# Threshold attention on one core: the spare products that keep the array's clock become single steps of a searched order, the start's warming products become smaller, and the order is searched on

## The chip, the cores and the metric

The kernel runs on 1 core of one Trainium2 chip. The metric is the device time of one execution in microseconds. The engines are PE (TensorE, the matrix products, with PEld for its weight loads), ACT (ScalarE), DVE (VectorE), POOL (GpSimd) and SP (SyncE, which here only issues DMAs). Each engine works through its own instructions in the order of the program; they wait for each other by semaphores.

## The reference

Q, K and V are float32 of 8 batches x 12 heads x 512 rows x 64. The weights of a row that are over a threshold of 0.1 are kept and divided by their sum, the others are zero:

```python
scores = np.einsum('bhqd,bhkd->bhqk', Q, K) * scale
weights = np.exp(scores - np.max(scores, axis=-1, keepdims=True))
weights = weights / (np.sum(weights, axis=-1, keepdims=True) + 1e-10)
weights = np.where(weights > threshold, weights, 0)
weights = weights / (np.sum(weights, axis=-1, keepdims=True) + 1e-10)
return np.einsum('bhqk,bhkd->bhqd', weights, V).astype(np.float32)
```

With 512 keys and a softmax over random scores, few rows have any weight over 0.1, and such a row mostly has one. The kernel is built on that.

## The kernel before

The 96 heads are taken as 48 pairs (`hp`), 24 groups of four heads (`hq`) and 12 groups of eight (`j`). The work has two parts.

The **body** looks in low precision for rows that might have a weight over the threshold. In the names that the planner and this text use:

- `k(hp)` and `q(hq)` load K (two DMAs from SP, L194) and Q (one DMA from POOL's queue, L209, which casts to f16). `z(hq)` clears four heads of the output in HBM with one DMA from SP (L324); every output row that is not written later stays zero.
- `ktr`, `kev`, `kf` transpose K on PE (L334), copy it from PSUM (L317 on ACT, L319 on DVE) and cast it to f16 (on POOL, L321). `qmix`, `qtr`, `qev` reorder Q (POOL L321 or DVE L319), transpose it (L367) and copy it back.
- `qk(hp, c)` (L377) makes a quarter of the scores of a pair, `exp(hp, c)` their exponentials, on ACT (L383) or by an integer trick on DVE (L385).
- `d(hp, jj)` (L389) and `dred` (L399, DVE) test whether a row has an exponential that is large against the row's sum.
- `ksq`, `qsq`, `size` (L357, L412) bound the rows' norms.

The **exact rows** are done once for each group of eight heads: `flags`, `rank`, `key`, `oh`, `idx`, `half`, `idxev` number the flagged rows, up to 32 in each pair of heads; `gather` fetches their Q rows from HBM by an indirect DMA of POOL (all indirect DMAs are at L190); `split` (L463), `xtr` (L469), `xev`, `xqk` (L481, exact scores in f32), `xexp` (L489), `tv`, `found` (L500) and `vidx` (L507) find the key; `vzero` (L514), `fetch` and `scatter` bring its V row and write it to the output. For the last group all this stands behind the last exp, as a chain. After the last group `check0` and `check1` (L535 to L541) decide whether a slow, complete path is needed; it is not for these inputs.

The **order** of all this is a table. Each step is added to a `Schedule` with the engines that may do it, an occupation and a latency for each, what it depends on, and which buffers it takes and gives. `ORDER` holds two strings: the first names the steps by pairs of digits in the order in which they are emitted, the second says which engine does a step that has a choice. An order search outside of the kernel wrote them. Each engine gets its steps in the order of the table, and nothing else orders the engines: on the chip a step starts when the engine reaches it and its semaphores allow it. The planner's dependencies that stand for no data (a `k` load behind `exp(hp - 6, 0)`, a clear behind a certain exp) are not waits on the chip.

Two things of the planner matter below. PSUM and the larger SBUF tiles are held buffers (`BUFS`: 3 of `sc`, 2 of `sm`, 7 of `kt`, 3 of `kf` and so on); the small tiles of the exact rows come from rotating pools (`small` with 6, `work` with 2), which the planner did not know of.

`spare(n)` emits n products of a zero tile with itself, 128x128 by 128x512, into the first `sc` buffer, that nothing reads. There are `WARM = 7` at the start, while the first loads are under way, and `HOLD = (0, 2, 8)` more: two behind `rank` of the last group and eight behind `xqk` of the last group but one.

```python
def spare(n, buf=held["sc"][0]):
    for i in range(n):
        at = slice(i % 2 * S, (i % 2 + 1) * S)
        keep(nc.tensor.matmul(buf[:, at], lhsT=warm[:, 0:P], rhs=warm[:], start=True, stop=True))
```

In the table of before, PE's order at the end is `d(47, 7)`, four `size`, `rank(11)` with two spares, `idx(11)`, `xtr(10)`, `xtr(9)`, `xqk(10)` with eight spares, `xqk(9)`, `xtr(11)`, `xqk(11)`. POOL's is `gather(9)`, `gather(10)`, `scatter(6)`, `split(9)`, `gather(11)`, `vzero(9)`, `scatter(7)`, `vidx(10)`, `vzero(10)`, `fetch(10)`, `vzero(11)`, `scatter(8)`, `fetch(9)`, `fetch(11)`, `scatter(10)`, `scatter(9)`, `scatter(11)`.

Of the kernel before, what the change touches and what calls it, by code (L numbers as in the profile page):

```python
# [55 lines left out]
def kernel(  # L56
# [59 lines left out]
    def by_pairs(ap):  # L116
# [9 lines left out]
    WARM = 7  # L126

    HOLD = (0, 2, 8)

    ORDER = (  # L130
        "04020001060D0B050t0u08070v2021090L0J0P0C0M0K0E220G0A0Q0F030s0H0r0y0+0N0a0c0O0b0d0x0R0S0T0U0V0z0W0X0Y0e0g102n2o0Z"
        "111c0-0h0f24121K2p1526281d25160i0j190k0l272B1A171R0m0n130o0p181S0q29142A1P1L1B1Q1M2T3y2s1C1N1D1E1O1F1G1H1I2W2E1T"
        "1U1V1W1X1Y1Z2X2F1a2C2r2t2a2D2u2l2m1J1b1e2v2b2y2w2I2J2x1f1g2G2U1h2V2H1i2-1j2Y332K2L2M2N2O2P2Q2R302Z343x4h3w0I4i1k"
        "1l4j3-413E1m2z312S1n1o3X3W2c2d433+2+32443H402e2f3F35363738393A3B3C3I424f3G3D5s1p453J3L4l2g3K2h4n2i462j3M4p4m4o4N"
        "1q4s582k3N3O3P3Q4847494C4A3R3S3T4q3U4D4B4r3V4S4O4U4E4F4T4P4V4G4H4I1r1s5q6b235r0w2q6c4J4v4K1t4L5D1u5v3Y4g5x6d1v4w"
        "4M5E5u4Q5z3Z5w4t3a3b3c4R1w5R5+3d5y4u3e1x1y5-6H1z3f4W4X5B4z4Y4Z4a4b4x3g1+5C4+3h6a3i4y605F4c4d594-5051615G4e525354"
        "5566645A6765565H5I5J5K5L6f625M5N5O6h6K5Q6Z6g576i5P636k6L6j3j7m8X5S6l68696A6B6C6D6I6O6M6E6F5T7K6G6m3k725U5V5W5X3l"
        "6J6P6N6n795Y3m7k8V7l4k8W3n7A5Z7p6o3o5a6r6t6p6s6q5b5c3p6u3q7r6Q7t6R7o6S7q6T77736U7s9g5d1-7v3r7u7L786V6W6v6X756w6x"
        "6y6z6+6-707476807w7y817x8a6Y717z8c3s8B3t5e7B7C7D7E7F7G7H7+7I8e8Z8C7-8D7J8f8b8G825f83848586875g8HAP9eAQ9f3z5h8889"
        "5i8d8U8T8A9j8g5m7M9l8I8E8l7N9n7O8J8F5jAR8y9o8j7P8h8m8k5k8i5l5nBa8z7Q8K8L8M8n7R8N8O8P8Q8R8-8+3u5o7S8S7T8o909i919k"  # L140
        "8p7U8q9m8r8sAT938t8u8v92949p8wAV9u9w9F7V7WANAU9E8x9vAWAX9x95969798999A9B9C7XA59D9q9sACAY9r9tAD9GAaAsAZ9H9IA8A69J"
        "9K9L9yAA9z9+A77nBZ5t8YBYCJCKA99M7Y9-AfAx7ZA0A1A2A3ABAyAgAO7aB89NA47bAhAbAv7cAiAEAFAGAH9OAIAJAKAdAcAwAeBcAtBeCLB9"
        "Bd3v9PBf9QAuDUBhALAzAMBiDSDTBgCNCPA+9RBjB-CO7dCICRAjAkAlAmBmBkA-AnBqB0B1B2BnBrAoB3C0B4B5B67eBl7gCQEFCU7f9SCmB7Bo"
        "C2ApAqCSC1BpArC3CTC6BsBtBuBvBwBxByBz9T9UCXCV9VCY9W9hEDEECM6eC77hDXBA9aDZ9XCWB+CHCZDWCpDYBBCaCqDa9YFO5p9ZDdDv9bBC"
        "BDC4BEBFCnCbDbC5BGD2DcBH7i9cCcCoC8C9CACBCCCtCDCECdCFCGCeCfDeDgCgBICuDfBJEIBKD3EKBLDiDhDjChCiEHCrEJCjCkEMClCsELDk"
        "DwCvCwCxCyENEODlCzC+C-D0D1DxEBE0ETDmDnDoD4EgE1EUDpD5D6D7EnEREoFNFMASG7G8EjDqDrDsDtD8ESEkDuFRG9BMEPD+BND9EVBOEQDA"
        "FTDBEzBPFVDyD-EWBQDzFWFQEhEiFSFUHGHHDCEXEYEZElGBEaGDEbEcEdEeEmEyBRDDGCDEBSBU7jHI9dFXGEDFFpBTEfGFEpEqFcFYFeGGECG5"
        "GHGIBVBWFdFZFfErEsFaEtEuEvEwE2FqE3E4E5FbExGsFrE6FsFwFgE7E8E9FhFiFjFkFlFmFnHLEAE+FoI3HNGaDGFxFtFuGJFvHPE-F0F1GbGN"
        "HQGKGOHKF2DHF3HMDIGcF4GfGPFyDJFzHOGQI1JBJAI2DKF5H-GgDLG6JCHRHjI6I8F+F-GLGhG0G1G2F6HUGMGiF7F8HVGdG3G4DMGeGRGSGTGU"
        "HSGVGWHYHkGjGkGlHTGXGmGYGnGoGpGqHoHlHZHpGtGZI5IAHmI7GrF9JzDODNIBI9JFGuJHICIUFAHnGvHWGwJJGxGyGzHqIFHXHrIGJKIDG+Im"  # L150
        "I0IEHaHbHcHdHeHfHgJEFBHhIXIVJGHiIWG-FCIYJIJyJxI4DVL5BbL4FDHsFEHtIJIHIZHuHvH0HwIKFFH1InH2IIIaFIBXDPK0JLJdL6H3K2Hx"
        "HyIbJiHzILIMINIOIPIQIRISJMIcJjFGFHH+JvFJJNITJQIdIeIfJgIgIhIiIjIkJ-FKDQJRJhIlIoLtJOK1JSK4IpJPK3K5IqJeJkIrK6JTJfJl"
        "IsJUJVJWJXJYJZJaJbKOLrL7LsJ+LuFPEGGAJDHJKPKBK9KQL9H4LBKgJwJcKAItJmJnJoJpJqJrJsJtK7KCIuJuL8KVK8LAKWLDH5KDLCKELFH6"
        "LEKTKRH7KUKSH8KFKGLGLILMKXKHKYKIKJKKKZKaKLKMKbKcLHLJLNLXLwHCH9LpKhHALqKNHBLyHDLvLKLxLLL+LYLzLZL-KdLaLeLOLPKeLQLc"
        "LRHELbKfLfM0MIKiLSLTLUM7MLLVKjMaIvLWLdM8MMKkKlM1M3IwKmKnM2M4IxKoKpIyM5MPLgLhLiLjLkLlLmLnKqMNLoM6MQKrMJKsMOM9IzKt"
        "DRI+MKMAMBMCMDMEMFMGMRMbMHMSMTMUMVMWMXMYMdMZMeMfMgMcMhMiMjKuMkKvMlMmKwI-KxM+J0KyKzJ1K+MnJ6FLMoJ2MpMqK-L0L1MwHFJ3"
        "MrL2J4J5J7MsMtMuJ8MvM-MxL3MyJ9Mz",
        "0000011111100000001100001000100000011011010000100000100110000010000000100101100101000100011001000000000100011000"
        "0100001100000101000011000100000000111000110101100001000101100001000100000111010000100100000010110000111000100001"
        "1100001001010000000101100000110110011000001000000010000000001110011000000001000010000000010010000100000000100010"  # L160
        "00001010001001100011001111",
# [14 lines left out]
    sched = Schedule(BUFS)  # L176
# [86 lines left out]
    spare(WARM)  # L263

# [212 lines left out]
    def do_xqk(j, eng):  # L477
        xq = T.pop(("xq", j))
        for n in range(4):
            sl = slice(n * SLOTS, (n + 1) * SLOTS)  # L480
            keep(nc.tensor.matmul(buffer("sm", ("xs", j))[sl, :], lhsT=xq[:, sl], rhs=pair("kt", 2 * j + n // 2)[:, n % 2],  # L481
                                  start=True, stop=True, tile_position=(0, n * SLOTS)))
        if j == NO - 2:
            spare(HOLD[2])
# [80 lines left out]
    for hq in range(NQ):  # L565
# [29 lines left out]
        for n, hp in enumerate(pairs):  # L595
# [31 lines left out]
        stage("flags", {"POOL": (0.25, 0.4), "DVE": (0.12, 0.3)}, [("dred", 4 * j + n) for n in range(4)] + ["casts"], do_flags)  # L627
        for n in range(4):
# [9 lines left out]
        stage("half", {"DVE": (0.08, 0.24), "ACT": (0.2, 0.36)}, [("idx", j)], do_half)
        stage("idxev", {"DVE": (0.13, 0.30)}, [("half", j)], do_idxev, gives=[("sm", ("ix", j))])
        stage("gather", {"POOL": (1.45, 4.2 if near else 6.4, 0.1)}, [("idxev", j)], do_gather)  # L640
        stage("split", {"POOL": (0.4, 0.55), "DVE": (0.21, 0.37)}, [("gather", j), ("half", j)], do_split)
        stage("xtr", {"PE": (0.17, 0.40)}, [("split", j)], do_xtr, takes=[("sm", ("xp", j))])
        stage("xev", {"DVE": (0.2, 0.35), "ACT": (0.2, 0.36)}, [("xtr", j)], do_xev, gives=[("sm", ("xp", j))])
# [121 lines left out]
```

## Time and profile before

| | |
|---|---|
| median of 3 runs | 201.56 us (200.13 to 201.98) |
| the profiled execution | 202.59 us |
| its span in the profile | 200.9 us |
| busy: PE, DVE, ACT, POOL | 180.6, 171.3, 165.5, 120.5 us |
| mean granted TensorE clock | 0.974 |
| DMA | 32.83 MB, 163 GB/s over the span |

Times in the profile count from the start of the span. The profiled execution is one of its own beside the three runs, 1.03 us over their median. Of a line of a timeline the first number is the start, the second how long it took, then engine, line of the kernel, operation, the tiles written and read, and how many instructions are merged; brackets give the engine's idle time before it and what ended it. SPq marks the issue of a DMA, not its transfer.

### The profile page before, as it was taken

To read this page: it belongs to the slowest core of one execution; us is meant where nothing else is said; L and a number is where in the kernel's file an instruction comes from. 1 tells how busy PE (TensorE), PEld (TensorE's weight loads), DVE (VectorE), ACT (ScalarE), POOL (GpSimd) and SP (SyncE) were. 2 spreads that over 40 slices of the span, in tenths; PEclk is the share of its full clock that TensorE was granted. 3 is DMA by queue.
4 is the path that set the end of the run, shared out by engine and by line. 5 is a ranking of instruction groups with operands and counts; after the bars stand their busy time and mean duration, and the time that the engine had idled before them with its cause. 6 is when DMAs were issued, how large, how long until landed. Compare 5 with 4: busy or idle time off the path is not lost. (4 is left out here: it accounts for less than half of the span.)

```text
span 200.9 us, 7649 instructions
## 1 busy us (share of the span) xinstructions
PE 180.6 (90%) x3190; PEld 119.7 (60%) x3191; DVE 171.3 (85%) x329; ACT 165.5 (82%) x197; POOL 120.5 (60%) x191
## 2 busy tenths in 40 slices
PE   7688999999999999999999999999999897988700
PEld 3355767666766677666677676657667654763100
DVE  6578989899999999999998999989999859888230
ACT  2799999899999899999899899899899797921200
POOL 5236366808668564829684859566878246165563
PEclk9999999999999999999999999999999999997875
DMA  5999999977886899989996676896789940000010
GB/s 130 195 240 200 235 226 261 271 124 185 117 148 175 295 226 149 233 113 272 194 215 128 104 119 154 106 274 135 212 206 352 363 120 8 3 11 5 8 16 9
DMA packets 69589, 32.83 MB, mean 163 GB/s; under 512 B 54355, under 2 KB 66277, under 8 KB 69552
## 3 DMA queue, kind: packets, MB, share of 16 engines
q1 hardware_dynamic: 55200, 25.44, 47.0%
q0 software_dynamic: 13296, 6.62, 25.7%
q8 instruction: 26, 0.43, 0.9%
q10 hardware_dynamic: 1056, 0.26, 0.6%
q14 instruction: 11, 0.09, 0.2%
HBM read 25.95 MB, written 12.98 MB: 194 GB/s over the span
## 5 line engine op out<-in xcount | busy, mean ns | idle before, releaser
L383 ACT ACTIVATE e<-sc 128x1024 bf16<-128x1024 f32 x143 | 137.3, 1035 | 7.3 <-PE sc L377 6.0
L389 PEld LDWEIGHTS <-e 128*128 128x128 bf16 x1536 | 51.6, 98 | 24.5 <-issue 22.8
L377 PE MATMUL sc<-qt,kf 64*128 64x512 f16 x384 | 63.4, 381 | 2.6 <-ACT qt L317 0.7
L389 PE MATMUL sm<-groups,e 128*128 128x64 bf16 x1536 | 61.9, 193 | 0.8 <-issue 0.6
L385 DVE TENSOR_SCALAR e<-sc 128x1024 int16<-128x1024 f32 x49 | 59.2, 1216 | 2.9 <-PE sc L377 2.2
L321 POOL CAST kf<-kt 128x512 f16<-128x512 f32 x46 | 28.6, 637 | 28.4 <-ACT kt L317 17.9
L399 DVE TENSOR_REDUCE stat<-sm 128x8 f32<-128x512 f32 x48 | 32.5, 682 | 3.5 <-PE sm L389 3.2
L377 PEld LDWEIGHTS <-kf 64*128 64x128 f16 x384 | 18.1, 94 | 15.1 <-issue 6.7
L190 POOL DMA_INDIRECT qsel<-in_Q_dram,idx x12 | 13.6, 1132 | 18.7 <-DVE idx L450 13.5
L321 POOL COPY qm<-q_sb 128x512 f16<-128x512 f16 x30 | 19.2, 650 | 2.3 <-DMA q_sb<-in_Q_dram 2.3
L334 PE MATMUL sc<-identity_f,k_sb 64*128 64x64 f32 x368 | 19.8, 228 | 0.6 <-ACT e L383 0.4
L209 POOL DMA_DIRECT2D q_sb<-in_Q_dram x23 | 19.1, 829 | 0.4 <-issue 0.3
L334 PEld LDWEIGHTS sc<-identity_f,k_sb 64*128 64x128 f32 x368 | 16.5, 138 | 4.4 <-ACT e L383 1.2
L489 ACT ACTIVATE xe<-sm 128x512 f32<-128x512 f32 x12 | 7.3, 606 | 12.0 <-PE sm L481 10.7
L190 POOL DMA_INDIRECT vsel<-in_V_dram,vidx x12 | 13.4, 1118 | 5.3 <-issue 1.8
L367 PE MATMUL sm<-identity_h,qm 128*128 128x128 f16 x184 | 14.2, 220 | 1.4 <-DVE stat L399 1.4
L190 POOL DMA_INDIRECT out_dram<-vsel,idx x12 | 12.9, 1071 | 3.3 <-issue 3.0
L317 ACT COPY kt<-sc 128x1024 f32<-128x1024 f32 x14 | 14.2, 1016 | 0.5 <-PE sc L334 0.3
L367 PEld LDWEIGHTS <-qm 128*128 128x128 f16 x184 | 10.6, 97 | 5.2 <-issue 4.6
L481 PE MATMUL sm<-kt,xq 128*32 128x512 f32 x96 | 12.9, 609 | 0.6 <-ACT xe L489 0.5
L357 DVE TENSOR_SCALAR qsq<-qt 128x1024 int16<-128x1024 int16 x24 | 12.9, 541 | 0.1
L319 DVE COPY qt<-sm 128x1024 f16<-128x1024 f16 x17 | 11.6, 684 | 0.9 <-PE sm L367 0.7
(94 smaller groups left out, 188.0 us busy)
## 6 DMA issues: line engine op xcount, KB each, us to landing
out_dram<-zero SPq DMA_DIRECT2D x24, 512.0 KB, 4.7
k_sb<-in_K_dram SPq DMA_DIRECT2D x95, 128.0 KB, 4.7
q_sb<-in_Q_dram POOLq DMA_DIRECT2D x23, 256.0 KB, 5.4
k_sb<-in_Q_dram SPq DMA_DIRECT2D x3, 128.0 KB, 3.7
qsel<-in_Q_dram,idx POOLq DMA_INDIRECT x12, 3.6
vsel<-in_V_dram,vidx POOLq DMA_INDIRECT x12, 3.3
out_dram<-vsel,idx POOLq DMA_INDIRECT x12, 3.6
k_sb<-in_K_dram ACTq DMA_DIRECT2D x1, 128.0 KB
```

Of the source, the lines that this page charges most:

```text
L190: return keep(nc.gpsimd.indirect_dma_start(**args))
L209: keep(nc.gpsimd.dma_start(out=q_sb[:].rearrange("p h r d -> p h (r d)"), in_=Q4[hq]))
L317: keep(nc.scalar.copy(dst, src))
L321: keep(nc.gpsimd.tensor_copy(dst, src))
L334: keep(nc.tensor.matmul(buffer("sc", ("ktr", hq))[:, at:at + D], lhsT=k_sb[rows, r, :, :].rearrange("p h d -> p (h d)"), rhs=identity_f32[ ...
L357: keep(nc.vector.tensor_scalar(buffer(which + "sq", hq)[:].bitcast(i16), buffer("kf" if which == "k" else "qt", hq)[:].bitcast(i16), 0x7FF ...
L367: keep(nc.tensor.matmul(buffer("sm", ("qtr", hq))[:].bitcast(f16)[:, at], lhsT=buffer("qm", hq)[:, at], rhs=identity_h[:], is_transpose=Tr ...
L377: keep(nc.tensor.matmul(buffer("sc", ("qk", hp, c))[:, h * S:(h + 1) * S], lhsT=pair("kf", hq)[ps, n, c * P:(c + 1) * P], rhs=pair("qt", h ...
L383: keep(nc.scalar.activation(e[:], sc[:], ACTF.Exp, scale=scale))
L385: keep(nc.vector.tensor_scalar(e[:].bitcast(i16), sc[:], BITS_A, BITS_B, op0=ALU.mult, op1=ALU.add))
L389: keep(nc.tensor.matmul(buffer("sm", ("d", hp))[:, j * G:(j + 1) * G], lhsT=buffer("e", (hp, c))[:, j * P:(j + 1) * P], rhs=groups[:], sta ...
L399: keep(nc.vector.tensor_reduce(T["stat", j][:, n, :], buffer("sm", ("d", hp))[:].rearrange("p (c g) -> p c g", g=G), axis=AX.X, op=ALU.max))
```

## The change

- `WARM` is 5; 32 small products follow the five: 64 rows by 128 columns of weights, 64 columns moved, in turn on rows 0 to 63 and 64 to 127, into two places of the buffer.
- `HOLD` is 18: eighteen steps `spare(n)` of one product each, which the table may put anywhere behind `d(47, 7)`. The two and eight spares behind `rank` and `xqk` are gone, and with them the planner's dependencies of `xqk(10)` on `idx(11)` and of `scatter(10)` on `fetch(11)`.
- The planner now knows of the small tiles (`idx`, `half`, `vsel`, `oh`, `qb`, `xq`, `xe`) and of two waits for a reused buffer. This changes no instruction, only which tables are allowed.
- Both strings of `ORDER` are new.

What the new strings hold, decoded: 140 exps are on ACT and 52 on DVE (143 and 49 before); `qev` 5 on ACT and 18 on DVE (6, 17); `qmix` 36 on POOL and 10 on DVE (30, 16). In order, for the places where the text below needs it:

- SP's end: `k(46)`, `k(47)`, `z(14)`, `z(19)`, `z(18)`, `z(22)`, `z(12)`, `z(20)`, `z(21)`, `z(17)`, `z(16)`, `z(23)`. Before: `k(46)`, `z(22)`, `k(47)`, and then seven clears.
- POOL: `gather(8)`, `qmix(43)`, `q(22)`, `q(23)`, `flags(9)`, `kf(42)`, `vzero(7)`, `kf(43)`, `vzero(8)`, `split(8)`, `fetch(6)`, `qmix(44)`, `vidx(7)`, `qmix(45)`, `qmix(46)`, `fetch(5)`, `kf(44)`, `fetch(7)`, `tv(8)`, `kf(45)`, `qmix(47)`. Before: `q(22)`, `gather(8)`, `qmix(43)`, `vidx(7)`, `fetch(7)`, `flags(9)`, `q(23)`, `kf(42)`, `kf(43)`, `qmix(44)`, `split(8)`, `qmix(45)`, `kf(44)`, `kf(45)`, `qmix(46)`, `vzero(8)`, `tv(8)`, `vidx(8)`, `qmix(47)`, `fetch(8)`.
- POOL's end: `scatter(4)`, `scatter(2)`, `gather(9)`, `scatter(6)`, `scatter(5)`, `gather(10)`, `split(9)`, `gather(11)`, `scatter(7)`, `vzero(10)`, `scatter(8)`, `vidx(9)`, `vzero(9)`, `fetch(9)`, `fetch(10)`, `vzero(11)`, `fetch(11)`, `scatter(9)`, `scatter(10)`, `scatter(11)`.
- PE behind `xqk(8)`: `d(42, 0)` to `d(42, 2)`, `qk(44, 1)`, `ktr(46)`, `qk(44, 0)`, `ktr(47)`, the `d` of pairs 42 and 43.
- PE's end: `d(47, 7)`, four `size`, `rank(11)`, six spares, `idx(11)`, `xtr(9)`, one spare, `xqk(9)`, one, `xtr(10)`, one, `xqk(10)`, two, `xtr(11)`, two, `xqk(11)`, four, and one at the very end.

The diff, with the strings cut:

```diff
-    WARM = 7
-    HOLD = (0, 2, 8)
+    WARM = 5
+    HOLD = 18
     ORDER = (
...
     )
-    sched = Schedule(BUFS)
+    sched = Schedule({**BUFS, "idx": 6, "half": 6, "vsel": 6, "oh": 2, "qb": 2, "xq": 2, "xe": 2})
...
     spare(WARM)
+    for i in range(32):
+        rows = slice(i % 2 * D, (i % 2 + 1) * D)
+        keep(nc.tensor.matmul(held["sc"][0][:, i % 2 * S:i % 2 * S + D], lhsT=warm[rows, 0:P], rhs=warm[rows, 0:D], start=True, stop=True))
...
     # do_d
-        if (hp, j) == (NP - 1, C2 - 1):
-            spare(HOLD[0])
     # do_rank
-        if j == NO - 1:
-            spare(HOLD[1])
     # do_xqk
-        if j == NO - 2:
-            spare(HOLD[2])
...
-        stage("xqk", {"PE": (1.07 + 0.22 * HOLD[2] * (j == NO - 2), 1.27)}, [("xev", j)] + ([("idx", NO - 1)] if j == NO - 2 else []), do_xqk, takes=[("sm", ("xs", j))],
-              gives=[("kt", 2 * j), ("kt", 2 * j + 1)])
+        stage("xqk", {"PE": (1.07, 1.27)}, [("xev", j)], do_xqk, takes=[("sm", ("xs", j))],
+              gives=[("xq", j), ("kt", 2 * j), ("kt", 2 * j + 1)])
...
-        stage("scatter", {"POOL": (1.45, 3.35, 0.1)}, [("landed", j), ("z", 2 * j), ("z", 2 * j + 1)]
-              + ([("fetch", NO - 1)] if j == NO - 2 else []), do_scatter)
+        stage("scatter", {"POOL": (1.45, 3.35, 0.1)}, [("landed", j), ("z", 2 * j), ("z", 2 * j + 1)], do_scatter, gives=[("idx", j), ("vsel", j)])
...
+    for n in range(HOLD):
+        add(("spare", n), {"PE": (0.214, 0.3)}, [("d", NP - 1, C2 - 1)], 1000.0, lambda e: spare(1))
```

More of the change, by code (lines that the diff above doesn't have):

```diff
@@ L124 @@
     Oz = out.rearrange("b (hq h4) (p r) d -> (b hq) (h4 p) (r d)", h4=4, p=P // 4, r=4 * R)
-    WARM = 7
-    HOLD = (0, 2, 8)
+    WARM = 5
+    HOLD = 18
     ORDER = (
[L131 to L161, printed above, removed]
@@ L162 @@
+        "00001000011010011011011011",
     )
@@ L625, in stage @@
             add((name, j), engs, deps, x, lambda e: fn(j, e), takes=takes, gives=gives)
-        stage("flags", {"POOL": (0.25, 0.4), "DVE": (0.12, 0.3)}, [("dred", 4 * j + n) for n in range(4)] + ["casts"], do_flags)
+        stage("flags", {"POOL": (0.25, 0.4), "DVE": (0.12, 0.3)}, [("dred", 4 * j + n) for n in range(4)] + ["casts"] + ([("key", j - NS)] if j >= NS else []), do_flags)
         for n in range(4):
@@ L633 @@
                 gives=[("ksq", 2 * j + n // 2), ("qsq", 2 * j + n // 2)] if n % 2 else [])
-        stage("rank", {"PE": (0.2 + 0.22 * HOLD[1] * last, 0.43)}, [("flags", j), ("size", j, 3)], do_rank)
+        stage("rank", {"PE": (0.2, 0.43)}, [("flags", j), ("size", j, 3)], do_rank)
         stage("key", {"DVE": (0.18, 0.33)}, [("rank", j)], do_key, gives=[("sm", ("rk", j))])
-        stage("oh", {"DVE": (0.61, 0.78)}, [("key", j)], do_onehot)
-        stage("idx", {"PE": (0.51, 0.70)}, [("oh", j)], do_idx, takes=[("sm", ("ix", j))])
@@ L638 @@
[L638 to L643, printed above, removed]
@@ L644 @@
-        stage("xqk", {"PE": (1.07 + 0.22 * HOLD[2] * (j == NO - 2), 1.27)}, [("xev", j)] + ([("idx", NO - 1)] if j == NO - 2 else []), do_xqk, takes=[("sm", ("xs", j))],
-              gives=[("kt", 2 * j), ("kt", 2 * j + 1)])
-        stage("xexp", {"ACT": (0.58, 0.80)}, [("xqk", j)], do_xexp, gives=[("sm", ("xs", j))])
+        stage("oh", {"DVE": (0.61, 0.78)}, [("key", j)], do_onehot, takes=[("oh", j)])
+        stage("idx", {"PE": (0.51, 0.70)}, [("oh", j)], do_idx, takes=[("sm", ("ix", j))], gives=[("oh", j)])
@@ new lines @@
+        stage("half", {"DVE": (0.08, 0.24), "ACT": (0.2, 0.36)}, [("idx", j)], do_half, takes=[("half", j)])
+        stage("idxev", {"DVE": (0.13, 0.30)}, [("half", j)], do_idxev, gives=[("sm", ("ix", j))], takes=[("idx", j)])
+        stage("gather", {"POOL": (1.45, 4.2 if near else 6.4, 0.1)}, [("idxev", j)] + ([("split", j - NS)] if j >= NS else []), do_gather)
+        stage("split", {"POOL": (0.4, 0.55), "DVE": (0.21, 0.37)}, [("gather", j), ("half", j)], do_split, takes=[("qb", j)])
+        stage("xtr", {"PE": (0.17, 0.40)}, [("split", j)], do_xtr, takes=[("sm", ("xp", j))], gives=[("qb", j)])
@@ L647 @@
+        stage("xev", {"DVE": (0.2, 0.35), "ACT": (0.2, 0.36)}, [("xtr", j)], do_xev, gives=[("sm", ("xp", j))], takes=[("xq", j)])
+        stage("xqk", {"PE": (1.07, 1.27)}, [("xev", j)], do_xqk, takes=[("sm", ("xs", j))],
+              gives=[("xq", j), ("kt", 2 * j), ("kt", 2 * j + 1)])
+        stage("xexp", {"ACT": (0.58, 0.80)}, [("xqk", j)], do_xexp, gives=[("sm", ("xs", j))], takes=[("xe", j)])
         stage("tv", {"POOL": (0.22, 0.36), "DVE": (0.1, 0.28)}, [("xexp", j)], do_tv)
-        stage("found", {"DVE": (0.75, 0.95)}, [("tv", j)], do_found)
@@ L649 @@
-        stage("vidx", {"POOL": (0.22, 0.36), "DVE": (0.12, 0.28)}, [("found", j)], do_vidx)
-        stage("vzero", {"POOL": (0.12, 0.25)}, [("gather", j)], do_vzero)
+        stage("found", {"DVE": (0.75, 0.95)}, [("tv", j)], do_found, gives=[("xe", j)])
+        stage("vidx", {"POOL": (0.22, 0.36), "DVE": (0.12, 0.28)}, [("found", j)], do_vidx, gives=[("half", j)])
+        stage("vzero", {"POOL": (0.12, 0.25)}, [("gather", j)], do_vzero, takes=[("vsel", j)])
         stage("fetch", {"POOL": (1.45, 1.5)}, [("vidx", j), ("vzero", j)], do_fetch)
```

32 lines of the change are left out of this document (31 added, 1 removed).

## The prediction

> **What bounds the kernel now.** First the page's slices: they show which stretches are full. From slice 5 to 31 PE, DVE and ACT stand at 9 with few 8s, so the exps (143 on ACT, 49 on DVE) and the products that feed them fill the time. Two places are not full: slices 32 to 34 (156 to 171 us), and everything behind the last exp, from 177.5 us on.
>
> ```profile
> span 200.9 us, 7649 instructions
> PE   7688999999999999999999999999999897988700
> DVE  6578989899999999999998999989999859888230
> PEclk9999999999999999999999999999999999997875
> DMA  5999999977886899989996676896789940000010
> ```
>
> Each digit stands for five microseconds. Then the timelines of the two queues that load and clear, around the first gap:
>
> ```profile
> 146.99 8.61 SPq L324 DMA_DIRECT2D out_dram<-zero  x7
> ...
> 147.48 0.81 POOL L209 DMA_DIRECT2D q_sb<-in_Q_dram  x1
> ...
> 150.32 0.67 POOL L321 COPY qm<-q_sb 128x512 f16<-128x512 f16 x1
> ...
> 153.25 0.85 POOL L209 DMA_DIRECT2D q_sb<-in_Q_dram  x1
> ...
> 161.23 1.18 POOL L321 CAST kf<-kt 128x512 f16<-128x512 f32 x2 [4.08 <-ACT kt L317]
> 164.68 0.62 POOL L321 COPY qm<-q_sb 128x512 f16<-128x512 f16 x1 [2.28 <-DMA q_sb<-in_Q_dram]
> ```
>
> Behind the last K load nothing holds SP back, and it issues the seven zero clears that are left in a row (1.23 us each). The last Q load, q(23), is issued into them at 153.25 and its first reader, qmix(46), starts at 164.68: 11.4 us, against 3.7 in the quiet stretch 112 to 117. The DMA view of 158 to 162 shows why:
>
> ```profile
> q1 hardware_dynamic: 312, 1.13, 75.2%
> q0 software_dynamic: 410, 0.21, 37.6%
> ```
>
> (packets, MB, share of 16 engines). The clears take 0.28 MB/us and leave q0 0.0525 MB/us, so a Q load (256 KB) takes 5.0 us there. PE pays 1.42 us for it, before qtr(23) at 167.52. Last the timeline and the windows of the tail:
>
> ```profile
> 183.76 3.42 PE L261 MATMUL sc<-warm 128*128 128x512 bf16 x8
> ...
> 185.47 0.29 DVE L463 TENSOR_TENSOR qb<-qsel,half 128x128 f32<-128x128 f32 x1
> ...
> 187.12 1.06 PE L481 MATMUL sm<-kt,xq 128*32 128x512 f32 x8
> ...
> 188.12 0.33 PE L469 MATMUL sm<-identity_f,qb 128*128 128x128 f32 x1
> ...
> 192.87 1.01 POOL L190 DMA_INDIRECT vsel<-in_V_dram,vidx  x1 [1.39 <-DVE oks L541]
> ```
>
> ```profile
> 178.70:183.48 4.78, 3.44 (x59) 2.00 (x58) 3.64 (x10) 0.00 (x0) 1.70 (x3) 1.00 0.03 6
> 183.48:186.90 3.42, 3.42 (x12) 1.04 (x8) 2.06 (x6) 0.69 (x2) 1.87 (x5) 0.50 0.03 7
> ```
>
> In the windows' rows the last three numbers are granted clock, DMA share and GB/s. The eight spare products fell into 3.4 us of half clock, at 0.427 each, and xqk(9) and xtr(11) stood behind them although qb for xtr(11) was ready at 185.76. The last group's chain (xtr, xqk, exp, found, fetch, scatter) ends the run: fetch(11) at 192.87 and 8.0 us more.
>
> **The change, part by part.** The sum is made against the profiled execution, 202.59 us (span 200.9 and 1.69 around it); the median of the runs is 201.56, so 1.03 is taken off at the end. Places and engines of steps are from the two tables, decoded.
>
> Start. Two spares less at 0.425 (weight loads at 1.68, 2.10, 2.53) put the end of the large ones at 3.40. No row shows 64-row products of 64 columns in bf16 at this clock. The d products (128x64) take 2.40 us for 64, 0.0375 each, at full clock: 32 are 1.2 us; at half clock 2.4, and 0.6 if the two row halves run together. The end is 4.0 to 5.8 against 4.24; I take 5.2. The K transposes (1.09) then end at 6.3, the Q ones (0.68), which could not start before 5.88 for their DMA, at about 7.0 against 6.56: **+0.3**, bounds 0 and +1.0 (a full queue of 2.4 us). The kf cast moves from ACT (0.59) to DVE (0.68), beside the Q transposes.
>
> Body work. ACT loses 3 exps (3 x 1.035), one qev (1.02) and one xev, and gains two halfs: -4.0. DVE gains 3 exps (3 x 1.216), one qev (0.68), and loses six qmix (0.385), flags, tv and halfs: +1.3. Shared out, -2.7 over two engines is -1.3 each. POOL takes six qmix (0.65), flags and tv, +5.0, hidden by its waits (17.9 and 10.4 us for kt alone); with that cover gone, kf and so qk would be late. The exps stand in nearly the same order. I take half, **-0.7**, bounds -1.3 and +0.7 (new small waits of the same size).
>
> The Q loads at the end of the body. Three things move together. (a) SP has ten clears behind k(47), not seven. k(46) is issued at 143.51 and k(47) behind it, so the clears go from about 146.0 to 158.3. (b) q(22) and q(23) now stand together on POOL behind qmix(43), which ended at 150.99: issued at 151.0 and 151.8, against 147.48 and 153.25. (c) POOL has kf(44) no longer ahead of qmix(46) but behind it and behind fetch(5); before, kf(44) ran at 161.23 and qmix(46) at 164.68. So q(23) now gates kf(44), the K half of the next sixteen exps, and PE has qk(44,1) ahead of ktr(46), ktr(47) and all of d(43). The clears hold 10 x 0.524 = 5.24 MB; at 0.28 to 0.37 MB/us from 150 on they last to about 166. q(22) begins 1.5 us after its issue in a quiet stretch (first bytes at 113.75 for an issue at 112.25); 11.4 less 6.8 (a load at the mean of 157 to 164, 0.27 MB in 7 us) is 4.6 within the clears. I take 3.0: 154.0. Two loads at 5.0 to 6.8 each, say 5.75, end at 165.5 (bounds 162.5 and 169.2). Then 0.5 to the reader, qmix(46) 0.62, fetch(5) 1.26 with its gap, kf(44) 0.64: 168.5, and qk(44,1) at 168.6 against 162.88, where the first qk of that pair ran: 5.7 us late. The old wait of 1.42 for qtr(23) goes, since qmix(46) is done by then. **+4.3**, bounds +1.3 and +8.0. That q(22) holds up qmix(44) to about 160 (155.23 before) is inside this wait. ACT cannot make it up: twelve exps and a kev from 169.0 are 13.4 us, to 182.4, against 177.5 before.
>
> Tail. Six spares stand between rank and idx of the last group: at full clock 0.214 each (half of 0.427), 1.28 from 180.03, so idx at 181.3, not 181.10, and gather(11) at 182.8 (182.55). Its data are there 2.9 to 3.6 later (split at 185.47; median landing 3.6). split(11) at 186.4 behind found(9), xtr(11) at 187.1 behind xqk(10) and two spares, xev, xqk(11) at 187.95 against 188.99. From there fetch(11) followed 3.88 later: 191.8. check1, whose L541 was the last release ahead of it while vidx was done at 192.09, is now behind it in the table: without that wait 191.3. POOL is free by then: four indirect DMAs at 1.32 (194.19 to 195.51) behind gather(11) end near 190. The two more scatters ahead of gather(10) put it at 179.3, not 176.72; split(10) waits for check0 on DVE to 184.3 anyway. **-1.3**, bounds -1.6 and +1.5 (all at half clock: six spares 2.56). The new pools in the planner and the removed dependencies issue nothing.
>
> Sum: 0.3 - 0.7 + 4.3 - 1.3 = +2.6: 205.2 for a profiled execution, **204.2 us** for the median.
>
> **The rivals.** *The loads come in time* (faster). If q(23) lands by 158.9, kf(44) ends by 161.9 as before and both waits are gone: 0.3 - 0.7 - 1.4 - 1.3 = -3.1, 198.5 us. For it: the page's median landing is 5.4, and q(22), issued at 147.48, was read without a wait at 155.23 beside the clears. Against: the 11.4 of q(23), and three clears more. The Trainium skill, "DMA: Bandwidth & Descriptors", section "Anatomy of one DMA — SWDGE (gpsimd) path", fits such a transfer as 2.0 us and its bytes over 436e3 per us, an estimate of 2.6 us for 256 KB, by which this rival's 198.5 would hold; this trace shows 3.7 in quiet and 11.4 in the clears.
>
> *Half a wait* (no change). At the low bound, q(23) done at 162.5, the body loses 1.3: 0.3 - 0.7 + 1.3 - 1.3 = -0.4, 201.2 us. For it: 5.0 us per load is what 158 to 162 shows, and first bytes came after 1.5 us once.
>
> *The clock goes with the wait* (slower still). PE would stand some 5 us before qk(44,1). In the tail a stretch of 4.78 us with few long products ended in 3.42 us at 0.50. Another 3.42 at half clock among full PE work costs up to 1.7, and more where the tail's spares meet it: 204.2 + 1.7 + 0.6 = 206.5 us. Against: the spares after it, and short products go on around the wait. The Trainium skill, "TensorE: Matmul & The Clock Gate", section "HAM oscillation — how this bites in real kernels", says that idle gaps over some 3.4 us bring half the clock; by it this rival's 206.5 would be the result.
>
> **How the numbers follow.** Forecast 0.48 (own range 202.4 to 206.0), in time 0.17, half a wait 0.22, clock 0.13. Within 1%, about what a measurement of this kernel can tell from no change, is 199.5 to 203.6. Faster: nearly all of the second, 0.16. Slower: the forecast but for its lower edge, and the fourth, 0.58. Same: 0.26. The range, 200.0 to 207.0, leaves out most of the second and the upper end of the late loads.
>
> **What would show it.** Right: in the changed profile POOL shows a wait of several us at L321 qm for DMA q_sb between 155 and 167, kf behind it, PE and ACT idle some 4 us at once, and a DMA row full to about 166. The last d ends 3 to 5 us later than 178.68, and fetch(11) follows it by 12.6 to 13.1 us, not 14.2. Wrong: kf(44) near 161, no PE gap there; or the first exp a microsecond late; or spares at 0.427.

## The result, and the profile after

After the change the kernel takes 215.72 us (median of 6 runs, 212.51 to 219.71); before, beside it, 201.75 us. The ratio is 1.0607, with a 95% interval of 1.0506 to 1.0708. Executions of one kernel come in a faster and a slower kind, and this ratio, like all that follow, compares the faster ones alone (213.5 us against 201.3 on average, 12.2 apart), while the profiled execution of after is one of the slower. The direction is the one forecast, the size is not: 204.2 us was forecast, at most 207.0. The profiled execution took 216.1 us with a span of 214.3, so 13.5 us more than before's 202.59, and these 13.5 are what has to be found.

First the slices of after, 5.36 us each:

```profile
span 214.3 us, 7745 instructions
PE   7779999999999999999698989899998539999820
DVE  5758999989999999999989999989999507966730
PEclk9979999999999999999969999999999966959985
DMA  6998985967459999887698471969899900000010
```

Counted from 0, PE and DVE have one deep hole, in slices 31 and 32 (166 to 177 us), where before had a shallow one, and PE a small one in slice 19 (102 to 107). The DMA row stands at 8 or 9 from slice 27 to slice 31, up to 171 us, and is empty behind it. PEclk, almost all 9 before, has a 7 in slice 2, a 6 in slice 20, 6 and 6 in slices 32 and 33, and a 5 in slice 35.

The timelines of SP and POOL around the hole, as in the prediction:

```profile
152.74 12.34 SPq L329 DMA_DIRECT2D out_dram<-zero  x10
...
156.07 1.71 POOL L210 DMA_DIRECT2D q_sb<-in_Q_dram  x2
...
166.25 0.60 POOL L326 COPY qm<-q_sb 128x512 f16<-128x512 f16 x1 [2.75 <-DMA q_sb<-in_Q_dram]
...
172.45 0.61 POOL L326 COPY qm<-q_sb 128x512 f16<-128x512 f16 x1 [4.75 <-DMA q_sb<-in_Q_dram]
173.26 1.10 POOL L191 DMA_INDIRECT vsel<-in_V_dram,vidx  x1 [0.20 <-POOL qm L326]
174.38 0.62 POOL L326 CAST kf<-kt 128x512 f16<-128x512 f32 x1
```

Ten clears are issued in one go, both Q loads fall among them, and POOL stands 2.75 us for q(22) and 4.75 us for q(23), with fetch(5) and kf(44) queued behind qmix(46). The view of the tile q_sb, of these two loads alone, tells how long after its issue each was signalled as landed, q(22) first (q(21), ahead of the clears, took 4.0):

```profile
DMA to landing us min/median/max: 10.1/12.8/15.5
```

PE's timeline shows who waits for kf(44), and the windows what follows (PE, PEld, DVE, ACT and POOL busy with their numbers of instructions, then granted clock, DMA share, GB/s):

```profile
175.05 0.61 PE L382 MATMUL sc<-qt,kf 64*128 64x512 f16 x2 [4.70 <-POOL kf L326]
```

```profile
173.30:180.10 6.80, 5.05 (x65) 3.70 (x66) 2.35 (x4) 3.08 (x4) 6.33 (x9) 0.50 0.07 9
...
186.90:193.70 6.80, 6.71 (x111) 5.76 (x112) 4.09 (x8) 3.27 (x5) 3.87 (x4) 0.51 0.05 11
```

There are two stretches of 6.8 us at half clock: one begins in the hole and outlasts it by 5 us, and the second lies over the last d products.

How late each pair is comes from the two traces: the mean start of a pair's four exps against that of the same pair before. Up to pair 26 it is about 1 us, then 4.3 (pair 30), 6.1 (35), 5.8 (41), 13.2 (44) and 12.9 (47); the last d ends at 193.79, not 178.68, so 15.1 late. So some 5 us are lost between pairs 27 and 36, where the forecast saw a small gain, 7.4 at the late Q loads, and about 2 behind pair 47, where the last half-clock stretch lies (0.6 in e_clears and f_all, which have none there). The tail gives 1.7 back: fetch(11) follows the last d by 12.5 us (14.2 before). 15.1 - 1.7 is the 13.5 but for 0.1.

In the tail the spares (L262 here) follow each other at 0.21 us, (1.45 - 0.38) / 5, full clock, as PE's timeline shows; POOL's shows that the last fetch still waits for check1 (L540):

```profile
194.99 1.45 PE L262 MATMUL sc<-warm 128*128 128x512 bf16 x6
...
202.39 1.06 PE L482 MATMUL sm<-kt,xq 128*32 128x512 f32 x8
```

```profile
206.26 1.00 POOL L191 DMA_INDIRECT vsel<-in_V_dram,vidx  x1 [0.69 <-DVE oks L540]
```

The loss between pairs 27 and 36 begins here, on DVE and POOL:

```profile
103.38 2.83 DVE L362 TENSOR_SCALAR ksq<-kf 128x1024 int16<-128x1024 int16 x1
...
125.78 1.97 DVE L499 SCALAR_TENSOR_TENSOR junk<-xe,tv,key_no 128x512 bf16<-128x512 f32 x1
```

```profile
102.75 0.81 POOL L210 DMA_DIRECT2D q_sb<-in_Q_dram  x1
103.54 0.64 POOL L326 CAST kf<-kt 128x512 f16<-128x512 f32 x1
104.10 0.18 POOL L513 MEMSET vsel<- 128x64 f32 x1
104.20 0.63 POOL L326 CAST kf<-kt 128x512 f16<-128x512 f32 x1
104.75 1.18 POOL L326 COPY qm<-q_sb 128x512 f16<-128x512 f16 x2
```

`ksq(13)` takes 2.83 us, where its kind takes 0.42, and ends 0.28 after an unbroken run of five POOL steps; `found(5)` takes 1.97 instead of 0.75 beside two casts; and `oh(7)`, at 137.03, takes 1.67 instead of 0.68. Before, the longest of the first kind was 0.96. PE's timeline shows the waits for DVE's copies queued behind the first two:

```profile
106.87 0.63 PE L394 MATMUL sm<-groups,e 128*128 128x64 bf16 x16 [1.94 <-DVE qt L324]
...
128.41 0.86 PE L394 MATMUL sm<-groups,e 128*128 128x64 bf16 x24 [0.89 <-DVE qt L324]
```

With 0.69 us at 117.89 and 0.60 at 138.75 PE waits 4.1 us for DVE between 98 and 142 us, where before has no wait over 0.4. The half clock of slice 20 (108.5 to 111.9) lies there too, but it isn't the main part: e_clears and e_kf, which have this part of the order unchanged and no half clock there, fall back by 4.8 and 4.2 us from pair 26 to pair 36, after by 5.7.

### The profile page after: what moved, and what is told of

It reads as the page before. It is cut to its first block, busy times and chain, and to the rows that moved or that the text cites. A ratio compares the mean times of both kernels' runs of the same rounds, so it can differ in the third digit from the quotient of the medians.

```text
span 214.3 us, 7745 instructions
## 1 busy us (share of the span) xinstructions
PE 187.0 (87%) x3229; PEld 125.3 (58%) x3229; DVE 176.5 (82%) x322; ACT 163.4 (76%) x194; POOL 125.2 (58%) x201
## 4 chain that ended last, share of the span: by engine, by line
PE 42%; DVE 14%; DMA 13%; POOL 13%; issue 12%; SPq 3%; ACT 2%; POOLq 0%; DVEq 0%
PE sm L394 15%; PE sc L382 14%; DMA q_sb<-in_Q_dram 5%; DVE e L390 5%; DMA out_dram<-vsel,idx 5%; PE sc L339 4%; PE sm L372 3%; POOL vsel L191 3%; POOL kf L326 3%; SPq L195 3%; DVE ksq L362 2%; DMA k_sb<-in_K_dram 2%; DVE stat L402 2%; PE sm L482 2%; POOL qm L326 2%
## 5 line engine op out<-in xcount | busy, mean ns | idle before, releaser
L388 ACT ACTIVATE e<-sc 128x1024 bf16<-128x1024 f32 x140 | 135.5, 1030 | 20.5 <-PE sc L382 19.1
L382 PE MATMUL sc<-qt,kf 64*128 64x512 f16 x384 | 65.8, 394 | 7.3 <-POOL kf L326 4.7
L394 PEld LDWEIGHTS <-e 128*128 128x128 bf16 x1536 | 55.0, 102 | 25.2 <-issue 24.5
L394 PE MATMUL sm<-groups,e 128*128 128x64 bf16 x1536 | 64.9, 199 | 3.3 <-DVE qt L324 2.8
L390 DVE TENSOR_SCALAR e<-sc 128x1024 int16<-128x1024 f32 x52 | 63.1, 1218 | 3.0 <-PE sc L382 2.4
L326 POOL CAST kf<-kt 128x512 f16<-128x512 f32 x46 | 29.9, 659 | 20.8 <-DVE kt L324 10.0
L382 PEld LDWEIGHTS <-kf 64*128 64x128 f16 x384 | 18.4, 95 | 19.5 <-issue 5.9
L326 POOL COPY qm<-q_sb 128x512 f16<-128x512 f16 x36 | 23.0, 645 | 10.2 <-DMA q_sb<-in_Q_dram 10.2
L339 PEld LDWEIGHTS sc<-identity_f,k_sb 64*128 64x128 f32 x368 | 17.7, 147 | 6.8 <-issue 2.2
L372 PE MATMUL sm<-identity_h,qm 128*128 128x128 f16 x184 | 14.7, 223 | 2.2 <-POOL qm L326 2.2
L499 DVE SCALAR_TENSOR_TENSOR junk<-xe,tv,key_no 128x512 bf16<-128x512 f32 x12 | 10.9, 912 | 5.6 <-POOL tv L494 5.5
L322 ACT COPY kt<-sc 128x1024 f32<-128x1024 f32 x14 | 14.2, 1014 | 1.5 <-PE sc L339 1.0
L362 DVE TENSOR_SCALAR ksq<-kf 128x1024 int16<-128x1024 int16 x24 | 14.5, 603 | 0.0
```

Source lines behind the costliest of these rows:

```text
L326: keep(nc.gpsimd.tensor_copy(dst, src))
L339: keep(nc.tensor.matmul(buffer("sc", ("ktr", hq))[:, at:at + D], lhsT=k_sb[rows, r, :, :].rearrange("p h d -> p (h d)"), rhs=identity_f32[ ...
L362: keep(nc.vector.tensor_scalar(buffer(which + "sq", hq)[:].bitcast(i16), buffer("kf" if which == "k" else "qt", hq)[:].bitcast(i16), 0x7FF ...
L372: keep(nc.tensor.matmul(buffer("sm", ("qtr", hq))[:].bitcast(f16)[:, at], lhsT=buffer("qm", hq)[:, at], rhs=identity_h[:], is_transpose=Tr ...
L382: keep(nc.tensor.matmul(buffer("sc", ("qk", hp, c))[:, h * S:(h + 1) * S], lhsT=pair("kf", hq)[ps, n, c * P:(c + 1) * P], rhs=pair("qt", h ...
L388: keep(nc.scalar.activation(e[:], sc[:], ACTF.Exp, scale=scale))
```

## The experiments

The kernels ran on several chips; each ratio is to before on the same chip, and times are medians of all executions. Before's medians were 202.52 us beside e_tail, e_clears, e_kf and e_locks, 202.15 beside e_both, e_best and e_start, 211.17 beside e_all, 210.32 beside e_clears_idx, and 202.31 beside the four whose names begin with f.

**The tail alone.** Before's body and start, after's order and single spares behind the last d:

```diff
 # before's table up to d(47, 7)
-spare(2) behind rank(11), spare(8) behind xqk(10), before's order
+after's order, 18 x spare(1)
```

> The body of before (its table up to the last d of pair 47, seven large warming products) and behind it the tail of after: eighteen single spares, its order, its engines. Theory: the loss lies in the body alone and the tail gains what the profiles show between the last d and fetch(11), 14.2 us before and 12.5 after, so this runs 1.0 to 2.0 us under before, about 200.2. Rival, the spares themselves cost (they delay idx and the exact products, or heat nothing): 201.5 to 203.

Measured: 200.6 us, ratio 0.991 (0.9844 to 0.9977). That is what the theory expected. In its profile fetch(11) follows the last d, which ends at 179.06, by 12.5 us, and the tail keeps the full clock, as the windows show:

```profile
178.94:191.55 12.61, 9.86 (x98) 4.01 (x95) 8.40 (x26) 2.34 (x7) 7.72 (x11) 1.00 0.04 8
```

So the tail is worth 0.9% by itself, and everything that is lost is lost ahead of it.

**The clears.** After, with seven of the ten last clears moved up on SP:

```diff
 # SP, in excerpts
 k(35)
+z(12), z(14)
 k(37)
+z(16), z(17)
 k(40)
+z(18), z(19), z(20)
 k(47)
-z(14), z(19), z(18), z(22), z(12), z(20), z(21), z(17), z(16), z(23)
+z(22), z(21), z(23)
```

> After, with seven of the ten clears behind k(47) moved forward on SP (two behind k(35), two behind k(37), three behind k(40)); nothing else. Theory: q(23) lands some 5 us after its issue and not 15, the 1.8 us wait of PE for qmix(44) and the 4.7 us for kf(44) go, and with them the half clock that follows: 6 to 8 us less than after, about 206 to 208. Rival, POOL's own order (kf(44) behind two more steps) makes the wait, not the clears: under 3 us less.

Measured: 208.37 us, ratio 1.0196 (1.0092 to 1.0301), so 0.041 below after, some 8 us. Its POOL timeline:

```profile
156.36 1.73 POOL L210 DMA_DIRECT2D q_sb<-in_Q_dram  x2
...
163.79 0.62 POOL L326 COPY qm<-q_sb 128x512 f16<-128x512 f16 x1
164.64 1.17 POOL L326 COPY qm<-q_sb 128x512 f16<-128x512 f16 x2
```

Neither `qmix(44)` nor `qmix(46)` waits for a load now. q(23) is signalled as landed 6.2 us after its issue, not 15.5. The theory's 6 to 8 us are there. The body's loss ahead of them is still there: pairs 35 to 41 are 6 us late, 2 of them since pair 3.

**The order of POOL at the hole.**

```diff
 # POOL
-qmix(46), fetch(5), kf(44), fetch(7), tv(8), kf(45)
+kf(44), kf(45), qmix(46), fetch(5), fetch(7), tv(8)
```

> After, with kf(44) and kf(45) ahead of qmix(46) on POOL; loads and clears as in after. Theory: q(23) is as late as in after, but PE can go on with qk(44) and the sixteen exps of the pairs 44 and 45 until it stands before qtr(23): the wait of 4.7 us shrinks to 2 or 3, so 2 to 3.5 us less than after. Rival, the late load does not bound: no change within 1 us.

Measured: 213.08 us, ratio 1.0498 (1.0421 to 1.0575), so 0.011 (2.2 us) below after, with intervals that overlap. The profile is clearer: kf(44) starts at 165.38, not 174.38, and pair 44 is 6.4 late, not 13.2; but pairs 45 and 46 are 9.2 and 10.7 late, since q(23) itself still takes 15.4 us. PE's wait has moved to qtr(23) (4.16 us, at 175.69) and has hardly shrunk, where 2 to 3 was expected. The cast behind `qmix(46)` is the smaller part of the hole; the late load is the larger.

**The blocked DVE steps.**

```diff
 # DVE
-ksq(13), found(5) where after has them
+ksq(13) behind exp(28, 0), found(5) behind exp(32, 1)
```

> After, with two DVE steps moved behind the exp that follows them: ksq(13), which took 2.83 us beside an unbroken run of POOL steps (0.42 otherwise), and found(5), which took 1.97 (0.75). Theory: DVE's step waits for the end of POOL's run and everything behind it on DVE waits too (PE 1.94 and 0.89 us for qt); moved, 2 to 4 us less than after. Rival, the long durations are filled from slack: within 1 us of after.

Measured: 214.24 us, ratio 1.0476 (1.036 to 1.0591): 0.013 below after, less than both intervals together can tell apart. The profile says why it can't be much. DVE's timeline:

```profile
103.55 2.52 DVE L431 TENSOR_TENSOR oh<-slot_no,keys 128x1024 f16<-128x1024 bf16 x1
```

`oh(5)`, now in that place on DVE, takes 2.52 us instead of 0.68. The block belongs to the place beside POOL's run, not to the step. So this edit frees `found(5)` (1.19 us) but not the longest block, and that holds for every kernel below that has the DVE moves: `oh(5)` takes 2.50 in each, and in f_all PE still waits 0.99 us for DVE behind it.

**Both, and what took the gain.**

```diff
+the seven clears of e_clears
+the two DVE moves of e_locks
```

> After with both repairs at once: seven of the last ten clears earlier, as in e_clears, and ksq(13) and found(5) out of the way of POOL's runs, as in e_locks. If the two losses are separate, their gains add: e_clears stands at 1.0196 of before, e_locks gained 2.6 us, so 208.4 - 2.6 = 205.8 by the times and nearer to 1.005 by the ratio; the last d some 2.5 us earlier than in e_clears (182.76), near 180.2. Rival: the blocked DVE steps cost only because a late Q load follows them; then nothing is gained beyond e_clears, ratio 1.02.

Measured: 207.69 us, no better than e_clears: the rival's number, though for another reason than the rival's. Up to pair 34 it is at most 1.9 late, then 7.1 at pair 36. The timelines of DVE and PE there:

```profile
139.97 0.28 DVE L451 TENSOR_SCALAR idx<-sm,slot_base,half 128x1 int32<-128x1 f32 x1 [3.63 <-DMA out_dram<-vsel,idx]
```

```profile
140.30 1.27 PE L394 MATMUL sm<-groups,e 128*128 128x64 bf16 x28 [3.52 <-DVE idx L451]
```

`idxev(7)` writes an index tile that a scatter still reads: `scatter(0)`, which issued at 60.4 in before, at 134.5 in after and at 131.55 in this kernel, just behind two Q loads, and was signalled as landed at 139.87. The body ran faster into a transfer that had not moved with it.

**The index tile.** `scatter(0)` goes directly behind `scatter(1)`, where its row has long landed:

```diff
 # POOL, its transfers alone
 gather(5), q(17), scatter(1)
+scatter(0)
 q(18), fetch(4), gather(6), fetch(3), q(19), q(20)
-scatter(0)
 fetch(2)
```

First on top of e_both:

> e_both with one step more moved: scatter(0), in after between q(20) and fetch(2), directly behind scatter(1). In e_both idxev(7) waited 3.63 us on DVE (139.97) for the index tile that the scatter at 131.55 still read, PE stood 3.52 us and half clock followed. Theory: the gain of e_locks was given back to this wait, so without it the exps from pair 36 on stand at +2 to +4 against before instead of +7, the last d near 181, and the time falls by 3 to 4.5 us from e_both (207.7), to 203.2 to 204.7, a ratio near 1.01. Rival: the next late transfer (the Q load behind it, or another scatter) takes its place and the ratio stays over 1.02.

Measured: 211.15 us, ratio 0.9993 (0.9958 to 1.0029). Then the same without the DVE moves:

> e_all without the two DVE moves: after with seven clears earlier and scatter(0) directly behind scatter(1); ksq(13) and found(5) where after has them. If the blocked DVE steps cost what e_locks gained from after (2.6 us) once the waits behind them are gone, the ratio is 0.012 to 0.013 over e_all's 0.9993, near 1.012. Rival: they are absorbed by the queues of exps ahead of PE and ACT, and the ratio stays within 0.005 of e_all's.

Measured: 213.89 us, ratio 1.0193 (1.0143 to 1.0243). The first is better than its theory (near 1.01), the second worse than its own (near 1.012). Since these two were on different chips, both ran again on one, with their partners that leave the ten clears in a row:

> e_all once more, on one chip with its neighbours: seven clears earlier, scatter(0) earlier, ksq(13) and found(5) moved. If the three terms account for the loss, the ratio is 0.995 to 1.005 again; if the chip made it, it is that of e_both, 1.02.

> The same without the two DVE moves. If the blocked DVE steps are worth what e_locks gained (0.013), the ratio stands 0.010 to 0.020 over f_all; if the step from 1.0193 to 0.9993 was the chip's, the two agree within 0.006.

> After with ksq(13) and found(5) moved and scatter(0) behind scatter(1), but the ten clears left at the end. By the terms: after's 1.061 less 0.013 for the locks and less 0 to 0.01 for the index tile, 1.040 to 1.048; if the locks are worth more once the index wait is gone, 1.035 to 1.040.

> After with scatter(0) alone moved behind scatter(1). idxev waited 0.50 and 1.02 us for index tiles in after, beside longer waits for Q: theory, no more than 1.5 us, ratio 1.053 to 1.061; rival, the scatter among the Q loads costs more than its own wait, under 1.05.

| on one chip | DVE moves | none |
|---|---|---|
| clears moved up | f_all 203.50, 1.0118 (1.0007 to 1.0229) | f_clears_idx 203.58, 1.0019 (0.9949 to 1.0088) |
| ten clears in a row | f_locks_idx 211.72, 1.0446 (1.0258 to 1.0634) | f_idx 210.64, 1.0422 (1.0266 to 1.0578) |

Read down: by the ratios the ten clears in a row cost 0.033 with the moves and 0.040 without, 6.6 and 8.1 us. Read across: the DVE moves are worth nothing that can be seen, so the 0.020 between e_all and e_clears_idx did not come again on one chip; with `oh(5)` held in the place of `ksq(13)`, this says nothing of what a free DVE would be worth. f_all lies between what its theory and its rival expected, f_clears_idx is 0.010 under f_all and not over it, f_locks_idx is within its theory, and f_idx is the rival's (under 1.05). The index tile: f_idx stands 0.019 below after and f_clears_idx 0.018 below e_clears, but f_locks_idx only 0.003 below e_locks, all across chips and with intervals that overlap or nearly do; 0 to 4 us is what these six ratios leave.

**The start alone.**

```diff
-WARM = 7
+WARM = 5
+32 small products in row tiles
```

> Before with after's start alone: five large warming products and 32 small ones in row tiles. In the profile of after they took 1.03 us and the first exp stood 0.1 us earlier. Theory: no change, -0.2 to +0.3 us. Rival: the small products do not keep the clock up, a half-clock stretch follows at 12.9 us as in after, and the whole body is 1 us later (ratio 1.005).

Measured: 202.39 us, ratio 1.0028 (0.9983 to 1.0074): no change. The 32 products take 1.04 us in all, and its profile has no half clock in the body, nor have e_kf and e_locks, with the same start, any near 12.9 us, so after's stretch there (slice 2) is not shown to be the start's.

**DVE beside POOL, by itself.** A POOL cast triggers the DVE step; n more casts are queued behind the cast:

```diff
+for op in (int16 SBUF, int16 from PSUM, two-input f32, f16 copy, f32 cast):
+    for n in (0, 1, 2, 4, 6): one POOL cast, n POOL casts, op behind the first
```

> Not the computation: five DVE operations, each beside 0, 1, 2, 4 and 6 back-to-back POOL casts of 0.6 us that were queued ahead and started just before it. Theory (a DVE step that needs the port pair waits for the end of POOL's whole run): the int16 step on SBUF (0.42 alone) takes 0.6 us more for each cast, some 3.6 to 4 us beside six; the f32 two-input one and the f16 copy the same; the int16 step that reads PSUM stays at 1.22. Rival (the two share the port cast by cast): no DVE step takes over 1.2 us, whatever the length of the run, as in before (largest 0.96).

The theory failed. Timelines of DVE (the int16 step on SBUF, and the one that reads PSUM) and of POOL, n = 6 for the first and n = 6 for the second:

```profile
16.61 0.81 DVE L672 TENSOR_SCALAR X<-E 128x1024 int16<-128x1024 int16 x1 [2.17 <-POOL Y L691]
...
29.30 1.23 DVE L675 TENSOR_SCALAR X<-sc 128x1024 int16<-128x1024 f32 x1 [1.56 <-POOL Y L691]
```

```profile
16.53 3.59 POOL L693 CAST Y<-W 128x512 f16<-128x512 f32 x6
...
29.21 3.40 POOL L693 CAST Y<-W 128x512 f16<-128x512 f32 x6
```

The SBUF step takes 0.80 or 0.81 for each n from 1 to 6, 0.42 alone: it waits for the cast in progress and then gets its turn, and POOL's six casts pay 0.19 for it. The step that reads PSUM stays at 1.23. The f32 step goes from 0.75 to 1.06, the f16 copy from 0.29 to 0.67.

So I swept the start of the step across the start of a run of four such casts:

> Not the computation: the int16 DVE step on SBUF (0.42 alone) beside a run of four back-to-back POOL casts, its start swept in steps of 0.05 us across the start of the run: eleven times with two small POOL memsets ahead of the run, fourteen times with the issue of a Q load ahead of it, as in after at 102.75. m_lock showed that a step that starts 0.1 us into a cast waits for that one cast alone (0.80), whatever is queued behind. Theory: a step that starts in the last 0.3 us before the run, so that both ask at once, loses every turn and waits for the whole run (over 2 us), in both families. Rival 1: this needs the DMA issue ahead of the run; only the second family shows it. Rival 2: no phase shows over 0.9 us, and the 2.83 us in after has another cause.

No phase gave over 0.84 us: rival 2. One thing was new: a step that started 0.16 to 0.51 us into POOL's issue of a Q load took longer too, from 0.82 down to 0.47, and always ended 0.24 after that issue's end. Then the same sweep with the steps that POOL has in after:

> Not the computation: the int16 DVE step swept again, in steps of 0.04 us, across the end of POOL's own DMA issue, now with the runs that blocked it in after: a Q load and then kf, a memset, kf and two f16 copies in qmix's pattern; the same without the memset; an indirect gather and then two casts; ahead of it on DVE a step from PSUM to SBUF. Theory: the mix of a DMA issue and a run of these very steps blocks the DVE step for the whole run (over 1.5 us) in at least one phase. Rival: as in m_phase nothing takes over 0.9 us, so that these steps alone don't do it and the cause of the 2.83 us in after stays open.

This time the theory holds, in one family. The run without the memset (cast, cast, copy, copy behind a Q load's issue), DVE and POOL:

```profile
119.07 2.05 DVE L672 TENSOR_SCALAR X<-E 128x1024 int16<-128x1024 int16 x1
```

```profile
118.36 0.75 POOL L733 DMA_DIRECT2D q_sb<-in_Q_dram  x1 [0.27 <-issue]
119.10 1.18 POOL L707 CAST Y<-W 128x512 f16<-128x512 f32 x2
120.22 1.36 POOL L704 COPY Y<-qx 128x512 f16<-128x512 f16 x2
```

In all six phases from 0.07 us ahead of the run to 0.11 us into it the step took 1.90 to 2.09 us: it got its turn only between the two copies. Earlier phases, 0.11 to 0.41 us ahead of the first cast, ran in 0.42 to 0.64. With a memset between the casts it was let in ahead of the second cast (0.96), in after it wasn't. Behind a gather and beside two casts, as `found(5)` stands in after, no phase took over 0.92, so the 1.97 of `found(5)` was not made again. A DVE step can be held over several POOL steps, then; at which of POOL's boundaries it is let in stays open.

**A version that beats both.** Before's body with its own clears spread, and after's tail:

```diff
 # e_tail's table
 k(35)
+z(15), z(16)
 k(37)
+z(17)
 k(39)
+z(18), z(20)
```

> Before's body and start with its clears spread (z(15) and z(16) behind k(35), z(17) behind k(37), z(18) and z(20) behind k(39)), and after's tail with its single spares. If the late q(23) of before costs the 1.42 us that PE waits for qtr(23), and the tail gains the 1.6 us of e_tail, the ratio to before is 0.984 to 0.988 (198 to 199 us). Rival: the clears that are moved up delay K loads there, and the gain of the tail is all that is left, 0.991, or less.

Measured: 199.9 us, ratio 0.9931 (0.9896 to 0.9965), the same as e_tail: the rival's number, 0.984 to 0.988 was hoped for. Its profile shows what was to be gained (pair 45 is 0.5 late where pair 41 was 2.4, so the wait for qtr(23) is gone) and what hid it: from pair 4 on it was 2.5 late, behind waits for the first K loads (0.55 and 0.66 us on PE), which before's profile doesn't have.

## Why the prediction was right or wrong

The forecast failed in its body term, and in its clock, which it left out of the sum; the Q loads, its largest term, came out much as worked out.

- **Body work, -0.7 with an upper bound of +0.7.** This step failed, in its sign: about +5 us by pair 36. The reason given was that POOL takes six qmix, flags and tv, +5.0, "hidden by its waits", with late kf and qk as the price should that cover be gone. PE does not wait for a kf ahead of the late Q loads. What it has is 4.1 us of waits for DVE (1.94 the longest), behind DVE steps that took 2.83, 1.97 and 1.67 beside unbroken runs of POOL steps. The prediction did not look at DVE beside POOL. It also compared POOL's orders from `gather(8)` on only, and `scatter(0)`, 74 us later than before, was in no term; e_both shows that it can stop DVE for 3.63 us. That the loss passes through DVE is what the traces show; what causes it is not shown by experiment. The DVE moves left a step of 2.50 in the same place. Moving either these or the scatter brings the ratio from 1.061 to 1.042 or 1.048, both together no further, and with everything moved f_all still falls back by 2.0 us from pair 26 to pair 36, f_locks_idx by 3.4. How the 5 us divide stays open.
- **Late Q loads, +4.3 with an upper bound of 8.0.** The mechanism was right in each step: ten clears in a row, POOL's `qm` wait, kf(44) behind it, PE and ACT idle 4.7 us. The wait was sized well too. From the issue of q(22) to `qmix(46)` it had 15.0 us (151.0 to 166.0); after has 16.4 (156.07 to 172.45), and e_locks and f_locks_idx, with the same ten clears, have 14.8 and 14.7. It had qk(44) 5.7 late by this wait; qk(44) runs 12.2 late (175.05 against 162.88), of which pairs 42 and 43 had 5.9 and 6.4 already. That all of it came 5 to 6 us later than the forecast's clock times is the body's loss ahead of it. The two loads did not share the time as supposed, 5.75 each: they landed 10.1 us and 15.5 us after their issues. What failed in this term is "the old wait of 1.42 for qtr(23) goes": the wait went, but pair 47 is still 12.9 late where pair 44 was 13.2, with half clock from 173.3 to 180.1 in between. The 6.6 and 8.1 us of the two pairs that differ in the clears alone hold the wait for qtr(23) as well, which those with the clears moved up do not have; the forecast's figure for that is 4.3 + 1.4 = 5.7. The Trainium skill, "DMA: Bandwidth & Descriptors", section "Anatomy of one DMA — SWDGE (gpsimd) path", gives an estimate of 2.6 us for such a load; 3.7 to 4.0 in quiet, 6.2 for q(23) with the clears moved up and 15.5 in the clears are what these runs show.
- **The clock.** Held as a rival of its own (206.5, one stretch of 3.42 us). It came together with the forecast's wait, and as two stretches of 6.8 us. That a chance was put on "the wait" and another on "the wait and the clock" was the wrong division: a PE gap of 4.7 us is both. All five profiles with the ten clears in a row have a PE wait of 4.2 to 4.8 us there and two stretches of 3.4 or 6.8 us at half clock. The rule that the prediction cited for the gap (the Trainium skill, "TensorE: Matmul & The Clock Gate", section "HAM oscillation — how this bites in real kernels") agrees with these. With the clears moved up the gap went, and the profiles of e_clears, f_clears_idx and f_all show no half clock between 120 us and the end of the body. But e_both and e_all, with the clears moved up too, have a stretch from 178.3 and 178.8 with no PE wait over 0.7 us in the 30 us before it, so a gap is not the only way to it.
- **Tail, -1.3.** Right in the main: -1.7 in after's profile, 1.8 by e_tail's ratio, with the spares at full clock. Its price for check1 was not: by the profile L540 was still the last release ahead of fetch(11), and POOL stood 0.69 us. How the 1.7 divides between the clock and the order of the steps was not tried apart.
- **Start, +0.3.** No cost: e_start is within its interval of no change. The 1 us by which pairs 2 to 26 are late in after is not the start's: in f_idx, with the same start, it is -0.4 to 0.7, in e_best, with before's, 2.5. It differs from one execution to the next with the first K loads.

## What to carry to other kernels

An engine's spare time is not free for work that uses what another engine needs: when steps move to an idle queue, look at what they run beside, and at the longest unbroken run that results. A transfer that has slack today (a clear, a scatter that holds a small rotating tile) should be placed while the queues are half empty; left to the end, it meets the last load that matters, and a faster body only runs into it sooner. In these profiles each PE wait of 3.5 us or more in the body (six of them) had half clock behind it, so such a wait and the slower clock behind it belong into the same sum, not into two cases.

## What the runs showed of the hardware

- A DVE step that reads and writes SBUF waits for the POOL step in progress: 0.80 for 0.42 us, 0.67 for 0.29, 1.06 for 0.75; one that reads PSUM (1.23) does not. The Trainium skill, "SBUF — State Buffer", section "Who interferes with whom", says that the two share a pair of ports and that the holder keeps it for its whole instruction; m_lock agrees. A step can also stay locked out over several POOL instructions in a row: over three in m_phase2 (2.05), beside five in after (2.83).
- Half clock came in stretches of 3.4 or 6.8 us and did not end with the gap: in after from 173.3 to 180.1, of which PE was busy 5.05 us, and again from 186.9 to 193.7 with PE busy 6.71 us, mostly on short products. PE waits of 1.0 to 2.0 us near 107 were followed by a 3.4 us stretch in some profiles (after, f_idx, f_clears_idx, f_locks_idx) and not in others (e_clears, e_kf, f_all). What starts such a stretch under a busy PE was not tried.
- A 256 KB Q load from POOL's queue took 3.7 to 4.0 us in quiet and 15.5 among clears of 512 KB from SP; from 164 to 172 us SP's queue had 77.3% of the engines' time and POOL's 18.4%.
